# A decoder step on one core: the down projection of pair 0 of the second and third token group is computed from seven products in place of eight

## The chip, the cores and the metric

The kernel runs on one core of a Trainium2 chip. The metric is the device time of one execution in microseconds (us); less is better. TensorE is called PE here, its weight loads PEld, VectorE DVE, ScalarE ACT, GpSimd POOL; SP is the queue from which nearly all transfers (DMAs) are issued.

## What is computed

One layer of a hybrid decoder for 2048 prompt tokens and 8 sample tokens of width 1024: a norm, one input projection, a gated linear recurrence and a sliding-window attention side by side, one output projection, and then the part that matters here, the feed-forward layer with its residual and a last norm:

```python
hn = _rmsnorm(h, norm2_g)
ff = jax.nn.silu(jnp.einsum('btd,df->btf', hn, w_gate)) * jnp.einsum('btd,df->btf', hn, w_up)
y = h + jnp.einsum('btf,fd->btd', ff, w_down)
...
y_prompt = _rmsnorm(yp, final_norm_g)
```

`w_gate` and `w_up` are 1024 x 2816, `w_down` is 2816 x 1024, all fp32.

## The kernel before, in words

**Arithmetic.** Every fp32 operand of a large matmul is split into a high part (`hi`, a cast by ACT to fp32r) and the rest (`lo`, a subtraction by DVE or POOL), and a product is three matmuls: hi x hi, hi x lo, lo x hi. A "product" below means these three, over however many 128-wide pieces of the contraction it has.

**Tiling of the feed-forward layer.** The 2056 tokens are cut into three token groups `gi` = 0, 1, 2 (first, second, third) of 688, 684 and 684 tokens, each of two halves `n` of 344 or 342 (`HALVES`, L35). The 22 slices of 128 of the inner width are taken as 11 pairs `p` = 0 to 10 (`NPAIR`). For every group and pair, `products` (L1360) computes gate (`x` = "g") and then up ("u") as a 2 x 2 block product (two slices by two token halves, the contraction cut in two as well) in Strassen-Winograd form: seven block products in the order `PRODS` = 1, 2, 6, 5, 7, 3, 4, each 12 matmuls, in place of eight. The four blocks of gate go through silu, those of up are multiplied with them; that gives the blocks `(h, n)` (slice h, half n) of the activation, in the tiles `c_u` (pool `gpb`, four buffers, so those of one pair).

**The down projection of a pair** adds its share to the group's result `y` (8 output slices `m` by two halves `n`, in SBUF). It exists in two forms, and `wino(gi, p)` (L77) chooses:

- `down` (L1449): eight products. For each of 16 `(m, n)` two slices x three matmuls, 96 matmuls in all, into a PSUM bank `pd`, and one DVE addition (L1469) into `y`: 16 additions. Its weights are four quarters of 128 x 512 (`down_weights` L1283: a load of 256 KB, a cast by ACT at L1224, a subtraction by POOL at L1225), its activations the four blocks, split by `part` (L1380 ACT, L1381 DVE) into `fh`/`fl`.
- `down_parts` (L1478): seven products, in 14 "rounds" `n` (two per weight tile, order `DPRODS` = 1, 5, 6, 3, 7, 2, 4 for the output slices of half 0, m = 0, 1 and 4, 5, then again for m = 2, 3 and 6, 7). A round is 2 x 3 matmuls into banks `pw` and two DVE additions (L1500): 84 matmuls and 28 additions. Products 1 and 6, then 7, then 4 add up in the same two banks (X), 5 and 3 in two others (Z); 2 has its own. Before the next product may be added to a bank, the addition that reads the bank must be done. Product 1 and 2 go into the y of m = 0, 1 and half 0; 6 and 3 into m = 0, 1 and half 1; 5 and 7 into m = 4, 5 and half 1; 4 into m = 4, 5 and half 0. Seven activations are needed: T1, T2, T3 are blocks, T5, T6, T7, T4 are made from them (L1399, L1402, L1403, L1406) by POOL or DVE (`E_T1`, `E_T2`). T1, T2, T3, T5 are split into the `fh`/`fl` tiles, T6, T7, T4 into two tiles `t`.
- The weights of the seven-product form are made in the second group by `down_make` (L1299: loads of the quarters, sums of them at L1326 by POOL or DVE as `E_DSUM` says, then `split_parts` L1291: cast L1293, subtraction L1294 by `E_DLO1`), and five of the seven tiles are also stored to DRAM (`sums_d`, L1343), from where `down_load` (L1345) takes them in the third group.

In the kernel before, the first group uses eight products for every pair; the second and third use seven for pairs 1 to 9 and eight for pairs 0 and 10.

**Storage around a change of group.** The pool `bigp` has 16 buffers (L303), each of three pieces of 344 columns. A group needs eight of them for a part of its input (`hn`), six for `y` (16 pieces), and two for its `t` tiles. The next group's `y` (loaded from DRAM by `y_load`, L1214 to L1220, in the order m = 0 n = 0, m = 0 n = 1, m = 1 n = 0, ...) and its `t` tiles can only move into buffers that have been left: those of `hn` after its last product, those of the old `y` when `finish` (L1502) has normalised it (L1520, DVE) and its store `out_yT` (L1521) has landed. Both run during pair 1 of the next group.

**What sets the order.** Each step is a Python generator that yields the planned time at which it is due; `plan` (L81) computes these times for the feed-forward layer: 1.764 us per product (`U_M`), 13.927 us for a `down` (`U_D`), 0.875 us per round (`U_R`). In `plan`, the `down` of pair p - 1 stands between gate and up of pair p; where pair p - 1 has seven products, its rounds stand two behind each product of pair p from the third on (`R_AT` = 2, counted from zero). The planned times are priorities: within them, an instruction takes its place on its engine when its operands and buffers are there in a modelled timeline. A written-out order of PE (`PE_ORDER`) covers all up to pair 1 of the first group and nothing behind it.

Of the kernel before, what the change touches and what calls it, by code (L numbers as in the profile page):

```python
# [36 lines left out]
NPAIR = NF // 2  # L37
# [13 lines left out]
T_B0 = 558.156  # L51
T_H3, D_H3 = T_B0 + 38, 4.0
DPRODS = [1, 5, 6, 3, 7, 2, 4]
U_R, R_AT = 0.875, 2
L_RW, L_DR, L_DS = 14.919, 18.881, 9.266
F_LEAD = [9.424, 18.27, 9.0, 0.611, 1.375, 5.911, 3.831, 7.271, 0.408]
F_HN = [23.685, 18.407, 28.406]
# [17 lines left out]


def wino(gi, p):  # L77
    return gi > 0 and 0 < p < NPAIR - 1


def plan():  # L81
    t, begin, end, prod, down, rounds = T_B0, [], [], {}, {}, {}
    for gi in range(len(HALVES)):
        begin.append(t)
        for p in range(NPAIR):
            mixed = p and wino(gi, p - 1)
            n = 0
            for i in range(14):
                if i == 7 and p and not mixed:
                    down[gi, p - 1] = t  # L90
                    t += U_D
                prod[gi, p, "gu"[i // 7], i % 7] = t - (U_D if gi and not p and i < N_EARLY else 0)
                t += U_M
                if mixed and i >= R_AT:
                    for n in range(n, min(14, n + 2)):
                        rounds[gi, p - 1, n] = t
                        t += U_R
                    n += 1
        down[gi, p] = t + (N_EARLY * U_M if gi < len(HALVES) - 1 else 0)
        t += U_D  # L100
        end.append(t)
    return begin, end, prod, down, rounds


T_B, T_END, T_PROD, T_DOWN, T_ROUND = plan()
AFTER = [
    ("xl2_5", "xc1_2_3"), ("xt3_1", "pth5_1_1"),
# [180 lines left out]
def hybrid_step(tc, xT, xR, vecs, cst, gatew, win, wout, wgate, wup, wdown, kT, vC, ck, cv, sconv, sh0,  # L288
# [4 lines left out]
    with ExitStack() as ctx:  # L293
# [884 lines left out]
        with ExitStack() as bctx:  # L1178
# [181 lines left out]
            def products(gi, p, x):  # L1360
# [9 lines left out]
                if not up:  # L1370
                    gss[gi, p] = C
                c11, c12, c21, c22 = (C[h, n][:, :nn] for h in range(2) for n in range(2))
                combine = up and wino(gi, p)
                if combine and gi not in extra:
                    place = slots(bigp, "big", f"t{gi}", F32R)
# [224 lines left out]
            for gi in range(len(HALVES)):  # L1600
                tb = T_B[gi]
                if gi:
                    ch.add(hn_mix(gi, stage, T_MIX[gi], F_MIX[2 * gi - 1]))
                    ch.add(hn_load(gi, PRODS[:3], slots(bigp, "big", f"hn{gi}_0", F32R), tb - F_HN[0], U_M))
                ch.add(hn_load(gi, PRODS[3:], slots(hnp, "hn", f"hn{gi}_1", F32R), tb - F_HN[1], U_M, None if gi else stage))
                ch.add(y_load(gi, tb + F_HN[2]))
                for i, n in enumerate((1, 0)):
                    te = T_END[gi]
                    ch.add(finish(gi, n, te + F_FIN[0] + F_FIN[1] * i, 1.0) if gi < 2 else finish_last(n))
                for p in range(NPAIR):  # L1610
                    ch.add(mixed_weights(wgate, gi, p, "g"))
                    ch.add(mixed_weights(wup, gi, p, "u"))
                    ch.add((down_load if gi == 2 else down_make)(gi, p) if wino(gi, p) else down_weights(gi, p, T_DOWN[gi, p]))
                    ch.add(products(gi, p, "g"))
                    ch.add(products(gi, p, "u"))
                    ch.add((down_parts if wino(gi, p) else down)(gi, p))
# [113 lines left out]
```

## Time and profile before

| | |
|---|---|
| time, three runs | 2064.38, 2058.54, 2060.22 us (median 2060.22) |
| span of the profiled execution | 2054.6 us |
| what lies around the span, against the median | 5.6 us |
| PE / PEld / DVE / ACT / POOL busy | 98% / 93% / 71% / 46% / 44% |
| matmul groups of the feed-forward layer | gate 489.4 us, up 479.9 us, down in eight products (`pd`) 239.4 + 153.4 us, down in seven (`pw`) 165.6 + 126.7 + 91.9 us (matmuls overlap, so these add up to more than the time they take) |
| granted TensorE clock, mean | 0.997 |

The trace has only the span of the profiled execution; the three times come from other executions. A row of the trace that groups instructions has the line, the engine, the operation, what it writes and reads, shape, count, then the busy time in us and the mean duration of one in ns, and behind the second bar the idle time of that engine just before them and what ended it. A row by stretches has for each engine its busy time and the number of instructions, then the granted clock, the share of time that the transfers keep the DMA engines busy, and their rate. A row of the timeline has start, length, engine, line, operation, names and count.

### The profile page before, as it was taken

What the parts mean: (1) busy time and instruction counts of PE and PEld (TensorE: products, weight loads), DVE (VectorE), ACT (ScalarE), POOL (GpSimd) and SP (SyncE); (2) the same over time, 40 slices, a digit from 0 to 9 for tenths busy, and PEclk for the clock granted to TensorE, in tenths of its full rate; (3) what the DMA queues carried; (4) which work ended last, traced back from release to release, by engine and by line L of the source; (5) the groups of instructions that cost most, each with busy time, mean ns of one, the idle gap of its engine ahead of it and who ended that gap; (6) DMA issues with size and microseconds to landing.
All of it is one profiled execution on the core that took longest, in us unless ns stands there. A gap on an engine that the chain in (4) does not pass through costs nothing.

```text
span 2054.6 us, 34857 instructions
## 1 busy us (share of the span) xinstructions
PE 2015.9 (98%) x12319; PEld 1908.1 (93%) x12319; DVE 1459.9 (71%) x2694; ACT 944.6 (46%) x1960; POOL 906.5 (44%) x799
## 2 busy tenths in 40 slices
PE   9999999999999999999999999999999999999998
PEld 9988787878777899999999999999999999999998
DVE  6877886767985766666654667777768666777675
ACT  6764774553664543343334533333335433433343
POOL 5311342020122787567656645556457522322333
PEclk9999999999999999999999999999999999999999
DMA  9864584576688856666546677776677675566652
GB/s 329 293 213 143 188 275 159 175 233 210 208 261 280 314 200 223 205 210 207 207 172 210 229 260 258 227 229 221 222 253 265 211 251 189 183 197 196 197 179 96
DMA packets 208991, 450.98 MB, mean 219 GB/s; under 512 B 25232, under 2 KB 82720, under 8 KB 208800
## 3 DMA queue, kind: packets, MB, share of 16 engines
q1 hardware_dynamic: 205184, 445.73, 65.2%
q10 hardware_dynamic: 3632, 3.02, 0.4%
q8 instruction: 97, 1.59, 0.3%
q14 instruction: 78, 0.64, 0.1%
HBM read 335.89 MB, written 113.84 MB: 219 GB/s over the span
## 4 chain that ended last, share of the span: by engine, by line
PE 77%; DVE 9%; DMA 6%; ACT 3%; issue 2%; POOL 1%; SPq 0%; DVEq 0%; ACTq 0%; POOLq 0%
PE ps_u L396 19%; PE ps_g L396 19%; PE pw L396 11%; PE pd L396 10%; PE ip L396 10%; PE op L396 4%; DMA n<-hs 3%; DMA xs<-in_xT 1%; DMA m<-mixed 1%; PE o L396 1%; PE pt L401 1%; DVE sc L974 1%; DVE sc L963 1%; PE s L396 1%; DMA mixed<-n 1%
## 5 line engine op out<-in xcount | busy, mean ns | idle before, releaser
L396 PE MATMUL ps_g<-hn,w_g 128*128 128x342 f32 (+1 forms) x2772 | 489.4, 320 | 4.6 <-DVE c_u L1410 1.8
L396 PE MATMUL ps_u<-hn,w_u 128*128 128x342 f32 (+1 forms) x2772 | 479.9, 319 | 1.9 <-ACT c_u L1436 1.3
L396 PEld LDWEIGHTS ps_g<-hn,w_g 128*128 128x128 f32 x2772 | 445.1, 188 | 6.0 <-DVE c_u L1410 2.3
L396 PEld LDWEIGHTS ps_u<-hn,w_u 128*128 128x128 f32 x2772 | 444.2, 188 | 2.6 <-ACT c_u L1436 1.6
L396 PE MATMUL ip<-xn,w_in 128*128 128x512 f32 (+1 forms) x1680 | 353.4, 358 | 1.9 <-ACT xn L431 1.8
L396 PEld LDWEIGHTS ip<-xn,w_in 128*128 128x128 f32 x1680 | 270.1, 189 | 46.0 <-issue 3.8
L1500 DVE TENSOR_TENSOR y<-y,pw 128x342 f32<-128x342 f32 x504 | 238.7, 504 | 73.0 <-PE pw L396 72.2
L396 PE MATMUL pd<-fh,w_d 128*128 128x344 f32 (+1 forms) x960 | 239.4, 320 | 0.6 <-DVE y L1469 0.6
L396 PE MATMUL op<-mix,w_out 128*128 128x512 f32 (+1 forms) x960 | 203.4, 357 | 0.5 <-DVE rrec L763 0.3
L396 PEld LDWEIGHTS op<-mix,w_out 128*128 128x128 f32 x960 | 155.4, 188 | 29.3 <-issue 5.0
L1469 DVE TENSOR_TENSOR y<-y,pd 128x344 f32<-128x344 f32 (+1 forms) x240 | 117.9, 507 | 75.3 <-PE pd L396 70.7
L396 PEld LDWEIGHTS pd<-fh,w_d 128*128 128x128 f32 x960 | 168.3, 188 | 1.4 <-DVE y L1469 1.1
L396 PE MATMUL pw<-fh,wd 128*128 128x342 f32 x576 | 165.6, 319 | 1.2 <-DVE y L1500 1.2
L396 PE MATMUL pd<-fl,w_d 128*128 128x344 f32 (+1 forms) x480 | 153.4, 320 | 0.0
L1381 DVE TENSOR_TENSOR fl<-c_u,fh 128x342 fp32r<-128x342 f32 (+1 forms) x132 | 107.1, 815 | 48.3 <-ACT fh L1380 47.9
L1225 POOL TENSOR_TENSOR w_u<-ru,w_u 128x512 fp32r<-128x512 f32 x44 | 58.9, 1338 | 181.6 <-ACT w_u L1224 155.0
L1392 POOL TENSOR_TENSOR c_u<-c_u,c_g 128x342 f32<-128x342 f32 (+1 forms) x60 | 60.5, 1008 | 170.7 <-DVE c_u L1410 132.1
L1380 ACT CAST fh<-c_u 128x342 fp32r<-128x342 f32 (+1 forms) x132 | 63.0, 480 | 157.8 <-POOL c_u L1392 61.9
L396 PE MATMUL pw<-t,wd 128*128 128x342 f32 x648 | 126.7, 320 | 2.6 <-DVE t L1381 1.7
L1410 DVE TENSOR_TENSOR c_u<-c_u,ps_u 128x342 f32<-128x342 f32 (+1 forms) x99 | 50.2, 507 | 100.3 <-PE ps_u L396 100.1
L396 PEld LDWEIGHTS pw<-t,wd 128*128 128x128 f32 x648 | 106.0, 188 | 4.4 <-DVE t L1381 2.5
L396 PEld LDWEIGHTS pw<-fh,wd 128*128 128x128 f32 x576 | 105.3, 189 | 1.7 <-DVE y L1500 1.5
(316 smaller groups left out, 3507.4 us busy)
## 6 DMA issues: line engine op xcount, KB each, us to landing
w_g<-split_g SPq DMA_DIRECT2D x88, 512.0 KB, 4.2
w_u<-split_u SPq DMA_DIRECT2D x88, 512.0 KB, 4.9
w_in<-split_w SPq DMA_DIRECT2D x84, 512.0 KB, 3.5
rg<-in_wgate SPq DMA_DIRECT2D x110, 256.0 KB, 3.1
ru<-in_wup SPq DMA_DIRECT2D x110, 256.0 KB, 3.2
w_out<-split_w SPq DMA_DIRECT2D x48, 512.0 KB, 4.4
split_g<-w_g SPq DMA_DIRECT2D x44, 512.0 KB, 3.6
split_u<-w_u SPq DMA_DIRECT2D x44, 512.0 KB, 2.7
```

The lines of the kernel that those rows point to most:

```text
L396: r = nc.tensor.matmul(*args, **kw)
L401: r = nc.tensor.transpose(*args)
L963: seen[f"sm{gb}_{kv}_{g}"] = nc.vector.tensor_tensor_reduce(sc[:, g, :kn], ps[:, gi * 256:gi * 256 + kn], mask[:, k0:k0 + kn], -SCALE, ns[ ...
L974: nc.vector.tensor_scalar(sc[:, g, :kn], sc[:, g, :kn], mx[:, 1, g:g + 1], None, ALU.mult)
L1225: lo_eng.tensor_tensor(w[:, 1, :], src, w[:, 0, :].bitcast(F32), op=ALU.subtract)
L1380: nc.scalar.copy(hi, v)
L1381: nc.vector.tensor_tensor(lo, v, hi.bitcast(F32), ALU.subtract)
L1392: (nc.vector if p == NPAIR - 1 or src is not v else eng(E_MUL[2 * h + n])).tensor_tensor(v, src, g, op=ALU.mult)
L1410: nc.vector.tensor_tensor(o, a, b, op)
L1469: r = nc.vector.tensor_tensor(ys[gi, n, m], ys[gi, n, m], ps, ALU.add)
L1500: nc.vector.tensor_tensor(v, v, ps, ALU.add)
```

## The change

`wino` now also holds for pair 0 of the second and third group, so these two `down` become `down_parts`, with all that belongs to it: `down_make` or `down_load` for their weights, the T activations in `products`, the rounds. In `plan`, the rounds of pair 0 stand behind the seventh to the thirteenth product of pair 1 (`R_FIRST` = 6), which puts the first of them at the planned time that the `down` had. All planned times behind them move forward, by 1.677 us per group.

```diff
-U_R, R_AT = 0.875, 2
+U_R, R_AT, R_FIRST = 0.875, 2, 6
...
 def wino(gi, p):
-    return gi > 0 and 0 < p < NPAIR - 1
+    return gi > 0 and p < NPAIR - 1
...
-                if mixed and i >= R_AT:
+                if mixed and i >= (R_AT if p > 1 else R_FIRST):
                     for n in range(n, min(14, n + 2)):
                         rounds[gi, p - 1, n] = t
                         t += U_R
```

## The prediction

> **What bounds the kernel now.** I read the page first, then the stretches by pair, then PE's waits, then the timelines of SP, DVE and PE around the change of group.
>
> ```profile
> span 2054.6 us, 34857 instructions
> PE 2015.9 (98%) x12319; PEld 1908.1 (93%) x12319; DVE 1459.9 (71%) x2694; ACT 944.6 (46%) x1960; POOL 906.5 (44%) x799
> ```
>
> PE is busy throughout, so a matmul removed is time removed, unless PE then waits. The span is 2054.6 us; against the median of the runs, 2060.22, there lie 5.6 us around it, which the change does not touch. I sum against the span and add the same 5.6.
>
> The stretches (start:end, length, then busy time and count of PE, PEld, DVE, ACT, POOL) of one pair with eight products (first group, pair 5), one with seven in its place (third group, pair 4), then pair 1 of the second and of the third group, where the change falls:
>
> ```profile
> 872.70:914.20 41.50, 41.50 (x265) 41.50 (x265) 28.48 (x42) 16.30 (x32) 26.93 (x20) 1.00 0.62 210
> 1742.10:1781.70 39.60, 39.60 (x255) 39.60 (x254) 27.86 (x52) 14.96 (x30) 11.54 (x10) 1.00 0.64 199
> 1166.70:1211.20 44.50, 44.50 (x297) 44.49 (x296) 26.00 (x49) 13.59 (x28) 16.22 (x16) 1.00 0.79 266
> 1620.80:1662.90 42.10, 42.10 (x278) 42.10 (x277) 25.82 (x51) 13.20 (x26) 11.43 (x10) 1.00 0.78 248
> ```
>
> PE never rests in any of the four, and its clock is full. Where PE does wait, second group and then third:
>
> ```profile
> PE pw L396 <- DVE y L1500: 2.0, 3, 1.2
> PE ps_g L396 <- DVE c_u L1410: 1.8, 2, 0.9
> PE pw L396 <- DVE t L1381: 1.7, 3, 1.1
> PE ps_u L396 <- ACT c_u L1436: 1.3, 1, 1.3
> ...
> PE pd L396 <- DVE y L1469: 0.6, 2, 0.3
> ```
>
> That is 6.8 us in the second group and 0.6 in the third, most of it behind DVE.
>
> **What goes: matmuls.** By the code a pair with seven products has 84 + 84 + 84 = 252 matmuls, with eight 264. 39.60 / 252 = 0.157 us each, and the first two stretches differ by 1.9 us = 12 x 0.157. The change does this in two groups: 2 x 1.9 = **-3.8 us**. [...]
>
> **What comes, engine by engine.**
>
> ```profile
> L1500 DVE TENSOR_TENSOR y<-y,pw 128x342 f32<-128x342 f32 x504 | 238.7, 504 | 73.0 <-PE pw L396 72.2
> L1469 DVE TENSOR_TENSOR y<-y,pd 128x344 f32<-128x344 f32 (+1 forms) x240 | 117.9, 507 | 75.3 <-PE pd L396 70.7
> L1381 DVE TENSOR_TENSOR t<-c_u,t 128x342 fp32r<-128x342 f32 x54 | 44.3, 829 | 3.3 <-ACT t L1380 3.3
> L1294 DVE TENSOR_TENSOR wd<-rd,wd 128x512 fp32r<-128x512 f32 x54 | 51.7, 957 | 2.7 <-ACT wd L1293 2.7
> L1225 POOL TENSOR_TENSOR w_d<-rd,w_d 128x512 fp32r<-128x512 f32 x60 | 86.3, 1446 | 25.2 <-ACT w_d L1224 24.8 <-POOL w_d L1225 0.4
> L1294 POOL TENSOR_TENSOR wd<-rd,wd 128x512 fp32r<-128x512 f32 x45 | 61.0, 1355 | 77.3 <-ACT wd L1293 63.2 <-DVE y L1500 12.4 <-DVE c_u L1392 1.7
> L1326 POOL TENSOR_TENSOR sd<-rd,sd 128x256 f32<-128x256 f32 x18 | 17.6, 976 | 0.8
> L1406 POOL TENSOR_TENSOR c_u<-c_u,c_u 128x342 f32<-128x342 f32 x18 | 19.3, 1074 | 12.1 <-DVE fl L1381 11.6
> ```
>
> DVE, second group: 28 additions in place of 16 (12 x 0.504 = 6.0), three more T remainders (3 x 0.829 = 2.5), three weight remainders (3 x 0.957 = 2.9), one sum (under 1): +12 us; third group about +13 (four weight remainders, one T). Pairs 0 and 1 hold it: in pair 1 alone DVE idles 44.5 - 26.0 = 18.5 and 42.1 - 25.8 = 16.3 us. POOL, second group: -4 x 1.446 + 4 x 1.355 + 7 x 0.976 + 4 x 1.074 = +10.7 us, beside 28.3 idle in pair 1; third about +1. ACT: three casts of weights and three of T more, about 3 us beside 30 idle. SP gets five more stores and six more loads (ten halves of a quarter in place of four quarters) in the second group, four more loads in the third, at about half a us each (eight stores take 5.10 and 4.13 below), spread over the 25 us ahead of the stores of y. In sum all of this is covered by idle time; each such us costs one if the cover is gone at the moment PE needs the result.
>
> **The wait that the change brings.** SP's loads of the new y, second group and then third:
>
> ```profile
> 1124.94 0.62 SPq L1220 DMA_DIRECT2D y<-hs  x1
> 1136.86 4.17 SPq L1220 DMA_DIRECT2D y<-hs  x5
> ...
> 1191.22 0.53 SPq L1343 DMA_DIRECT2D sums_d<-sd  x1
> 1193.28 0.80 SPq L1220 DMA_DIRECT2D y<-hs  x2
> 1194.13 5.10 SPq L1521 DMA_DIRECT2D out_yT<-y  x8
> 1199.31 0.42 SPq L1220 DMA_DIRECT2D y<-hs  x1
> 1200.34 3.26 SPq L1220 DMA_DIRECT2D y<-hs  x7
> ...
> DMA to landing us min/median/max: 1.9/4.1/4.7
> ...
> DMA to landing us min/median/max: 4.3/4.5/6.9
> ...
> 1644.53 4.13 SPq L1521 DMA_DIRECT2D out_yT<-y  x8
> 1648.93 3.39 SPq L1220 DMA_DIRECT2D y<-hs  x7
> ```
>
> Six pieces of y (m = 0 to 2) come early, ten only around 1193 to 1204, seven of them behind the store of the old y. (The two landing rows are those of the stores and of the loads.) PE is already at this down projection:
>
> ```profile
> 1178.64 0.32 PE L396 MATMUL pd<-fh,w_d 128*128 128x342 f32 x1
> ...
> 1633.30 0.32 PE L396 MATMUL pd<-fh,w_d 128*128 128x342 f32 x1
> ```
>
> Eight products use y in the order in which it comes, so only late additions wait. Seven products change that in two ways. First, the second round (product 5) adds into m = 4, 5 of half 1, the 10th and 12th piece; product 3 must follow it in the same banks, so round four stands until about 1205. Second, T6, T7 and T4 of pair 0 need the group's two t tiles now, one pair earlier, and the 16 buffers are taken (8 hn, 6 old y, 2 new y): the first comes when the first buffer of the old y is stored, 1191.1 + 4.1 = 1195, the second after the second store of the other block, about 1196 + 4.1 = 1200, and T7 is split some 2 us later, 1202. Till then `c_u` of pair 0 holds its buffers, and up of pair 1 gets no further than its fourth product, since products 7 and 3 need banks that are copied into `c_u`.
>
> What PE can do meanwhile from 1178.6: 48 matmuls of gate (7.5 us), norm matmuls (about 2), four products of up (7.5), rounds 1, 2, half of 6 (15 matmuls, 2.4) and round 3 (0.9), in sum 20.3 us, to about 1199. So PE waits 1199 to 1202: **+2.7 us**. Behind that lie three products of up and a round (6.6 us), which cover y of 1205. Bounds: 0 if the stores go out 3 us sooner (DVE no longer has to slip the old additions between the normalisations), 8 if T4 and the late y are waited for in full (1207). Third group: work from 1633.3 to about 1651, T7 at 1644.5 + 1 + 4.1 + 1.8 = 1651.4: **+0.4 us**, bounds 0 and 4. I take the middle estimates, since the rows of before place each step.
>
> Sum: 2054.6 - 3.8 + 2.7 + 0.4 = 2053.9 of span, with 5.6 around it **2059.5 us**. A measurement of this kernel can tell about 0.3% from no change, 6.2 us; -0.7 us lies well within.
>
> **The rivals.**
>
> Clean gain: PE finds work over the whole wait, as it does now (44.50 of 44.50 busy in that stretch although ten pieces of y are late). For it: the order behind the first group is not written out, and PE takes what is ready. Against it: the products of pair 2 need weight buffers that the standing rounds hold. 2060.2 - 3.8 = 2056.4 us.
>
> Slower: a jam at the change of group. T tiles, `c_u` buffers and late y hold one another, and when they come free at 1202 to 1207, some 24 additions, ten T remainders and the new weights fall on DVE at once, 12 + 8 + 5 us of DVE work before the 20 us of PE work that waits for it. Price: 8 + 4 for the full waits, 2 to 5 for the burst (the pairs of the second group that wait at all wait 1 to 3 us each), -3.8: 2070 us. It decides if the waits exceed 3.8 + 6.2 = 10 us. What DVE's share is worth depends on these rows:
>
> ```profile
> L1381 DVE TENSOR_TENSOR fl<-c_u,fh x132: 500/793/1658, 706.1 to 2026.1; 128x342 fp32r<-128x342 f32 x88, 128x344 fp32r<-128x344 f32 x44
> L1500 DVE TENSOR_TENSOR y<-y,pw x504: 494/503/515, 1220.6 to 2017.6; 128x342 f32<-128x342 f32 x168
> ```
>
> The addition from PSUM always takes 0.50, the remainder of two SBUF operands 0.50 to 1.66; ten remainders at the upper end are 8 us more. [...]
>
> Faster: the waits that the second group already has (6.8 us) fall otherwise once every later step has moved, and most of them go: 2056.4 - 3 to 6.8, about 2051 us. The stretches show no reason for it, only that such waits come and go from pair to pair.
>
> The change does not do what it says: the seventh product is only a planned time. The first pd ran when gate of pair 1 had four products to go. The rounds may be spread into pair 2, and the 12 matmuls saved all the same, 2056 to 2062 us.
>
> **How the numbers follow.** The forecast 0.42, clean gain 0.26, jam 0.18, faster 0.08, rounds elsewhere 0.06. The first, second and last lie within 0.3%: 0.74 the same. Of the jam nearly all is over 6.2 us: slower 0.17 (the rest goes to the same), faster 0.08, same 0.75. The range goes from 2054.5, just under the clean gain and what a run scatters, to 2067, the waits at their bounds without the burst and half of the jam: it leaves out the faster case and the upper half of the jam, under 0.2.
>
> **What would show it.** Right: 24 fewer matmuls in 2 x 1.9 us; pw from about 1178 and 1633 on; `t` tiles written from about 1196 and 1646; waits of PE of 1 to 5 us near 1199 to 1203, released by DVE or ACT on `c_u`; POOL longer by 10 us in the second group. Wrong: waits over 10 us between 1195 and 1230, or pairs 2 and 3 of the second group longer than 40 us by DVE; or no wait, and then the clean gain.

## The result, and the profile after

| | before | after |
|---|---|---|
| time, median (four runs each) | 2061.78 us (2058.54 to 2064.38) | 2091.91 us (2090.93 to 2093.09) |
| ratio after / before | | 1.0142, 95% interval 1.0125 to 1.016 |
| span of the profiled execution | 2054.6 us | 2090.9 us |

The change makes the kernel 1.4% slower, 30 us by the medians and 36.3 us by the two spans. The forecast was 2059.5 us, no change. (The ratios, here and below, differ a little from the quotient of the medians, which is 1.0146 here; the intervals are those of the ratios.)

The page of the profile after, its span and its busy times:

```profile
span 2090.9 us, 34921 instructions
PE 2026.9 (97%) x12295; PEld 1913.6 (92%) x12295; DVE 1483.5 (71%) x2733; ACT 948.9 (45%) x1972; POOL 921.4 (44%) x812
```

The work changed as forecast: 24 matmuls fewer (12319 to 12295), DVE 23.6 us longer (12 + 13 were counted), POOL 14.9 (11.7 counted), ACT 4.3. What grew is the time in which PE has nothing to do. The stretches after (length, then busy time and count of PE, PEld, DVE, ACT, POOL, then granted clock, DMA share, GB/s) of pair 1 and pair 2 of the second group and pair 1 of the third:

```profile
1169.80:1222.20 52.40, 44.18 (x276) 42.77 (x276) 32.31 (x55) 15.98 (x34) 23.71 (x23) 0.93 0.71 227
1222.20:1268.20 46.00, 43.45 (x263) 42.55 (x262) 35.38 (x63) 15.08 (x30) 26.98 (x26) 0.96 0.72 243
1649.60:1696.80 47.20, 41.58 (x251) 39.77 (x250) 32.79 (x62) 15.39 (x32) 14.66 (x12) 0.93 0.76 242
```

Pair 1 had 44.50 of 44.50 us busy before; now 8.2 of 52.4 us are idle, and in the third group 5.6 of 47.2. DVE is at 62% and 69% there, so it isn't full. PE's waits in pair 1, second group and then third:

```profile
PE pw L396 <- DVE y L1500: 7.1, 3, 4.7
PE ps_u L396 <- DMA w_u<-split_u: 1.1, 1, 1.1
...
PE pw L396 <- DVE y L1500: 5.6, 4, 1.8
```

PE waits for an addition into `y` that frees a bank, and for a weight of up. The addition in turn waits, as DVE's timeline in that stretch says (in brackets the idle time before the row and what ended it):

```profile
1204.23 0.51 DVE L1500 TENSOR_TENSOR y<-y,pw 128x342 f32<-128x342 f32 x1 [2.34 <-DMA y<-hs]
1207.19 0.51 DVE L1500 TENSOR_TENSOR y<-y,pw 128x342 f32<-128x342 f32 x1 [2.45 <-DMA out_yT<-y]
1209.68 1.55 DVE L1500 TENSOR_TENSOR y<-y,pw 128x342 f32<-128x342 f32 x3 [1.98 <-DMA y<-hs]
```

So the loads of the new `y` are late. SP's timeline shows how late, and what stands behind them:

```profile
1186.89 0.33 SPq L1248 DMA_DIRECT2D w_u<-split_u  x1
...
1189.82 4.83 SPq L1521 DMA_DIRECT2D out_yT<-y  x8
1194.77 1.34 SPq L1220 DMA_DIRECT2D y<-hs  x3
...
1196.63 3.96 SPq L1521 DMA_DIRECT2D out_yT<-y  x6
1201.72 2.23 SPq L1220 DMA_DIRECT2D y<-hs  x5
1203.99 0.90 SPq L1521 DMA_DIRECT2D out_yT<-y  x2
1204.94 4.84 SPq L1220 DMA_DIRECT2D y<-hs  x8
...
1210.35 0.85 SPq L1248 DMA_DIRECT2D w_u<-split_u  x2
...
1216.91 0.40 SPq L1248 DMA_DIRECT2D w_u<-split_u  x1
```

All 16 pieces of `y` come after 1194, where six came by 1141 before. And between the load of a weight of up at 1186.89 and the next ones at 1210.35 lie 23.5 us, filled with stores and loads that SP issues one behind another, loads of `y` among them that wait for stores of `y` (2.0 us in all); in the kernel before, four weights of up went out between 1188.12 and 1204.77, among the stores and loads of `y`. The first and the last of these four:

```profile
1188.12 0.40 SPq L1248 DMA_DIRECT2D w_u<-split_u  x1
...
1204.45 0.32 SPq L1248 DMA_DIRECT2D w_u<-split_u  x1
```

Of the 23.5 us, 18.1 are the issue of 16 stores and 16 loads of `y`, and for some 4 SP stands idle. What is late is the issue and not the transfer itself: the loads of `y` land 3.5 us after their issue here (2.7 to 4.1), where those of the same stretch took 4.4 before. Why `y` lost its early buffers is in the rows of the `t` tiles, before and after (count, then shortest/median/longest ns, first and last start):

```profile
L1380 ACT CAST t<-c_u x54: 461/479/482, 1221.0 to 1993.2; 128x342 fp32r<-128x342 f32 x54
```

```profile
L1380 ACT CAST t<-c_u x60: 462/480/483, 1180.2 to 2029.2; 128x342 fp32r<-128x342 f32 x60
```

The `t` tiles are first written at 1180, before any old `y` has been stored: they took the two buffers that `y` had. (e11 below gives these buffers back to `y` and so tests this.)

To add up where the time went I use the starts of all matmuls of the trace: where two of them in succession lie over 0.2 us apart, what exceeds the usual 0.158 us counts as a gap. A gap holds waits, and matmuls that run slower behind a wait (behind the 4.71 us wait of pair 1 they start 0.285 us apart for 3.4 us). By stretch, in us:

```
                                   before   after   difference
pair 1, second group                 0.3     11.4     +11.1
pair 1, third group                  0.3      9.6      +9.3
pairs 2 to 9, second group           8.3     23.4     +15.1
rest of the feed-forward layer      12.0     15.9      +3.9
sum                                 20.9     60.3     +39.4
```

39.4 less the 3.8 us of the matmuls is 35.6, and the spans differ by 36.3. So there are two places to explain: pair 1 of both groups (+20.4), and pairs 2 to 9 of the second group (+15.1), in which nothing was changed but planned times.

### The profile page after: what moved, and what is told of

It is laid out like the page before. It is cut to its first block, busy times and chain, and to the rows that moved or that the text cites. A ratio compares the mean times of both kernels' runs of the same rounds, so it can differ in the third digit from the quotient of the medians.

```text
span 2090.9 us, 34921 instructions
## 1 busy us (share of the span) xinstructions
PE 2026.9 (97%) x12295; PEld 1913.6 (92%) x12295; DVE 1483.5 (71%) x2733; ACT 948.9 (45%) x1972; POOL 921.4 (44%) x812
## 4 chain that ended last, share of the span: by engine, by line
PE 70%; DVE 10%; DMA 9%; ACT 3%; issue 3%; POOL 3%; SPq 1%; ACTq 0%; DVEq 0%; POOLq 0%
PE ps_u L396 17%; PE ps_g L396 16%; PE pw L396 10%; PE ip L396 9%; PE pd L396 9%; PE op L396 5%; DMA n<-hs 4%; DMA mixed<-n 1%; DMA out_yT<-y 1%; DVE n L521 1%; PE o L396 1%; PE s L396 1%; PE pt L401 1%; DVE sc L963 1%; DMA rd<-in_wdown 1%
## 5 line engine op out<-in xcount | busy, mean ns | idle before, releaser
L1500 DVE TENSOR_TENSOR y<-y,pw 128x342 f32<-128x342 f32 x560 | 265.1, 504 | 93.4 <-PE pw L396 77.8
L396 PE MATMUL pd<-fh,w_d 128*128 128x344 f32 (+1 forms) x832 | 206.6, 320 | 1.4 <-DVE y L1469 1.4
L396 PE MATMUL pw<-fh,wd 128*128 128x342 f32 x640 | 189.0, 327 | 10.3 <-DVE y L1500 10.1
L396 PE MATMUL pw<-t,wd 128*128 128x342 f32 x720 | 145.0, 326 | 15.4 <-DVE y L1500 9.5
L1469 DVE TENSOR_TENSOR y<-y,pd 128x344 f32<-128x344 f32 (+1 forms) x208 | 103.2, 508 | 65.6 <-PE pd L396 65.3
L396 PEld LDWEIGHTS pd<-fh,w_d 128*128 128x128 f32 x832 | 145.8, 188 | 1.9 <-DVE y L1469 1.6
L1381 DVE TENSOR_TENSOR fl<-c_u,fh 128x342 fp32r<-128x342 f32 (+1 forms) x132 | 105.5, 803 | 49.1 <-ACT fh L1380 48.5
L396 PEld LDWEIGHTS pw<-t,wd 128*128 128x128 f32 x720 | 120.0, 192 | 19.4 <-DVE y L1500 12.3
L396 PE MATMUL pd<-fl,w_d 128*128 128x344 f32 (+1 forms) x416 | 133.1, 321 | 0.0
L396 PEld LDWEIGHTS pw<-fh,wd 128*128 128x128 f32 x640 | 120.0, 193 | 13.1 <-DVE y L1500 12.9
```

The lines of the kernel that those rows point to most:

```text
L396: r = nc.tensor.matmul(*args, **kw)
L1381: nc.vector.tensor_tensor(lo, v, hi.bitcast(F32), ALU.subtract)
L1469: r = nc.vector.tensor_tensor(ys[gi, n, m], ys[gi, n, m], ps, ALU.add)
L1500: nc.vector.tensor_tensor(v, v, ps, ALU.add)
```

## The experiments

The theories, as they stood: **Y**: `y` is late since the `t` tiles take its two spare buffers. **D**: DVE is late with the additional additions, remainders and splits around pair 1. **Q**, formed after e8: beside `y`, the weights of up are late, because they stand in SP's queue behind the loads of `y`, which wait for stores. **N**, formed after e12: pairs 2 to 9 wait because the norm that prepares the third group's input keeps its planned time while the pairs move forward. All results are in this table; the gaps are those of the profiled execution, worked out as above (the column "pairs 2 to 9" is that of the second group). That is one execution of each kernel, and not always one near the median: 2101.52 us in e3, 2081.68 in e1. In pair 1 of the second group, kernels that are alike there agree within 0.5 us (0.3 in before, e2, e14, e16 and e17; 2.1 to 2.2 in e11, e13 and e18; 5.0 and 5.5 in e12 and e15).

```
                              time us    ratio    95% interval        gaps, us: pair 1   pairs    pair 1
                              (median)                               2nd group  2 to 9  3rd group
before                        2058.7 to 2062.5, by chip                 0.3       8.3     0.3
after                         2091.91   1.0142   1.0125 to 1.016       11.4      23.4     9.6
e1  second group only         2088.44   1.0120   1.0099 to 1.0142      11.2      21.6     0.9
e2  third group only          2070.05   1.0039   1.0024 to 1.0054       0.3      13.7     8.7
e3  no y                      2093.47   1.0157   1.0131 to 1.0183      10.8      25.3     9.7
e4  own t tiles               2094.78   1.0161   1.0143 to 1.018       10.0      24.8     5.5
e5  before, small pools       2080.84   1.0101   1.0084 to 1.0118       2.6      19.1     1.6
e6  own t tiles, y order      2098.31   1.0179   1.0163 to 1.0196      12.8      28.3     1.9
e7  rounds later              2088.53   1.0140   1.0122 to 1.0157      10.3      23.7     7.9
e8  y order                   2086.77   1.0128   1.0108 to 1.0147      13.7      16.9     9.1
e9  no y, y loaded later      2069.43   1.0035   1.0024 to 1.0046       0.3      16.5     2.5
e10 up's weights from ACT     2087.80   1.0121   1.0095 to 1.0146       5.0      23.2     8.9
e11 y first                   2082.52   1.0097   1.0078 to 1.0116       2.1      29.7     4.6
e12 e11, weights from ACT     2079.53   1.0087   1.0063 to 1.0111       5.0      21.3     2.5
e13 e11, norm earlier         2070.78   1.0049   1.0029 to 1.0069       2.2      21.8     1.3
e14 before, norm later        2071.73   1.0045   1.003  to 1.0061       0.3      15.9     0.3
e15 e12, norm earlier         2075.73   1.0070   1.0046 to 1.0093       5.5      20.6     2.2
e16 e2, y first               2065.71   1.0023   1.0006 to 1.0039       0.3      13.4     5.1
e17 before, norm earlier      2062.41   1.0013   0.9999 to 1.0027       0.3      10.1     0.3
e18 e13, norm earlier still   2068.52   1.0049   1.0036 to 1.0062       2.2      17.0     1.7
```

### e1 and e2: one group at a time

```diff
-    return gi > 0 and p < NPAIR - 1
+    return gi > 0 and (gi == 2) <= p < NPAIR - 1      # e1; e2 has (gi == 1)
```

In e2 the weights of pair 0 are made in the third group (`down_make`), since the second group has stored none.

> Pair 0 in seven products in the second group alone; the third group as before. Theory Y (PE waits for the new y, whose pieces come late because the two t tiles of pair 0 now hold the two spare buffers of the pool): the waits of pairs 0 to 2 of the second group stay (16 us, against 1 before), about +14 us after the 1.9 saved; the 11 us more of waits in pairs 4 to 9 of that group stay too if they follow from it, so 2075 to 2086 us, and the third group loses its 10 us of waits. Theory D (DVE has too much to do around pair 1): the same split, since both groups get the same DVE work; this run does not tell Y from D but says where the 30 us come from.

> Pair 0 in seven products in the third group alone, with its weight sums made there; the second group as before. If each group carries its own loss: about 10 us of waits against 1.6, less 1.9, so +8 us, 2068 to 2072 us; and pairs 4 to 9 of the second group wait 8 us as before. If those pairs wait 18 us here as well, the extra 11 us there do not come from the second group's pair 0.

The second group alone costs 2088.44 - 2061.48 = 27 us, the third alone 8.6. In e1 the waits are nearly those of the changed kernel: 11.2 us in pair 1 and 21.6 in pairs 2 to 9. In e2 they are 8.7 us in pair 1 of the third group. The third group has no later group whose input must be prepared, and nothing follows there: its pairs 2 to 9 have gaps of 0.0 in e2 as in the kernel before.

### e3: pair 0 doesn't add into y

```diff
-    nc.vector.tensor_tensor(v, v, ps, ALU.add)
+    if p:
+        nc.vector.tensor_tensor(v, v, ps, ALU.add)
+    else:
+        nc.vector.tensor_tensor(ps, hn[gi, 1, 0][0][:, :nn].bitcast(F32), ps, ALU.add)
```

> As changed, but the 28 additions of each pair 0 add a resident input tile to the bank and write it back there, in place of adding the bank into y; this leaves out the share of pair 0 of the second and third group in the result. The DVE instructions, their number and their place behind the matmuls stay; only y is no longer waited for. Theory Y: the waits in pair 1 and 2 go from 16 to under 4 us in the second group and from 10 to under 3 in the third, 2058 to 2068 us. Theory D: nothing goes, 2085 to 2093 us.

No gain at all: 2093.47 us, and 10.8 us of gaps in pair 1 of the second group. Theory Y by itself has fallen. But PE's waits of that stretch, second group and then third, name another culprit:

```profile
PE ps_u L396 <- DMA w_u<-split_u: 7.5, 1, 7.5
...
PE ps_u L396 <- DMA w_u<-split_u: 6.2, 1, 6.2
```

What was a wait of 1.1 us behind 7.1 us is now one of 7.5 us. Two things were late by nearly the same time, and the trace puts a wait down to the one that came last. SP's timeline of e3:

```profile
1192.63 0.33 SPq L1248 DMA_DIRECT2D w_u<-split_u  x1
...
1211.47 4.58 SPq L1220 DMA_DIRECT2D y<-hs  x8
1216.15 0.85 SPq L1248 DMA_DIRECT2D w_u<-split_u  x2
```

Nobody waits for `y` in pair 1 here, but its loads still stand ahead of the weights.

### e4, e5 and e6: own tiles for T6, T7 and T4

```diff
-    place = slots(bigp, "big", f"t{gi}", F32R)
+    place = slots(tsp, "ts", f"t{gi}", F32R, 3 * TP)     # e4, e6: tsp has 2 buffers
-rwp2 = B(tc.tile_pool(name="rwp2", bufs=4))              # e4, e5, e6: with 3 in rwp, a ring of 7 raw weights,
-wp2 = B(tc.tile_pool(name="wp2", bufs=3))                # and with 5 in wp one of 8 split weights
+rwp2 = B(tc.tile_pool(name="rwp2", bufs=2))              # 5 and 7
+wp2 = B(tc.tile_pool(name="wp2", bufs=2))
```

The two tiles are paid for with weight buffers; e5 is the kernel before with those small rings alone. e6 also loads `y` in the order in which the rounds want it (as e8).

> As changed, but the t tiles have two buffers of their own, so that the new y gets the two spare buffers of the pool again; to make room, the pools of raw and of split weights lose two buffers and one (7 to 5, 8 to 7), which the control run prices. Theory Y: six pieces of y come early again, ten at about 1195 to 1205; round two still waits for the 10th and 12th piece at about 1205 in place of 1209 to 1212: 5 to 8 us come back in the second group and 3 to 6 in the third, 2078 to 2084 us, plus what the smaller pools cost. Theory D: no change, 2090 us or more.

> Control: the kernel before with the smaller pools of raw and split weights (5 and 7 buffers), nothing else. All theories: what it is slower than the kernel before is the price of the smaller pools; 2060 to 2075 us.

> As the run with own t tiles, and y is loaded in the order in which the rounds use it (m = 0, 1 of half 0, m = 4, 5 of half 1, m = 0, 1 of half 1, m = 4, 5 of half 0, then the same with m = 2, 3, 6, 7), so that the six early pieces serve the first six rounds. Theory Y: PE has the first half of the rounds before the late pieces land; the waits of pair 1 fall below 4 us in the second group and 2 in the third, and the time comes to the control's less 0 to 4 us. Theory D: as the run with own t tiles.

As times these are lost: the small rings cost the kernel before 1.0%, and neither e4 nor e6 says what own tiles are worth in the second group. e6 was expected at the time of e5 or a little below; it came 17 us above. The third group can be read: its pair 1 goes from 9.6 us of gaps to 5.5 (own tiles) to 1.9 (and y order), where the rings by themselves (e5) leave 1.6. There Y holds. In the second group of e6 the wait is again `PE ps_u <- w_u`, 8.0 us.

### e7: the rounds behind the last products

```diff
-U_R, R_AT, R_FIRST = 0.875, 2, 6
+U_R, R_AT, R_FIRST = 0.875, 2, 9
-                    for n in range(n, min(14, n + 2)):
+                    for n in range(n, min(14, n + (2 if p > 1 else 3))):
```

The last round of pair 0 then stands behind the last product of pair 1, which has written its own T4 into the tile that both pairs share: the product 4 that goes into m = 6 and 7, half 0, is that of a wrong block. The work is the same in kind and number.

> As changed, but the rounds of pair 0 are planned three behind each product of pair 1 from the tenth on, in place of two from the seventh on: some 5 us later. Theory Y: PE does more products of up before it meets the rounds, if the buffers of c_u and of weights allow; 3 to 10 us come back, 2082 to 2088 us. Theory D: a denser burst of additions, no gain or a loss, 2090 to 2097 us. A third, that the planned place matters little since PE takes what is ready: within 2 us of the changed kernel.

The first round is planned three products later (5.3 us), and the ratio stays: 1.0140 for 1.0142. But the plan moved more than the rounds did. By the matmul starts, the first round of the second group still begins 14.5 us into pair 1, the second at 24.8 us (17.4 in the changed kernel) and the sixth, behind the long wait, at 41.7 (40.5). So this shift of the planned times brings nothing; it doesn't show that the place of the rounds is without weight.

### e8: y in the order of the rounds

```diff
-                for m in range(KD):
-                    yield t + m
-                    for n, (o, nn) in enumerate(HALVES[gi]):
+                first = ((0, 0), (1, 0), (4, 1), (5, 1), (0, 1), (1, 1), (4, 0), (5, 0)) if gi else ()
+                first += tuple((m + 2 * (gi > 0), n) for m, n in first)
+                for i, (m, n) in enumerate(first or [(m, n) for m in range(KD) for n in range(2)]):
+                    yield t + i // 2
+                    o, nn = HALVES[gi][n]
```

> As changed, with y loaded in the order in which the rounds use it and nothing else. Theory Y: the first pieces to land (three near 1198, the next from 1205) are then those that rounds one and two need; round two no longer waits for the 10th and 12th piece at 1209 to 1212 but for the 3rd and 4th: 5 to 12 us come back in the second group and 3 to 6 in the third, 2074 to 2084 us. Theory D: 2090 us.

A ratio of 1.0128, little less than after, and pair 1 of the second group even has 2.3 us more. PE's waits there:

```profile
PE ps_u L396 <- DMA w_u<-split_u: 7.0, 1, 7.0
PE pw L396 <- DVE y L1502: 3.0, 3, 1.9
```

The wait for `y` has shrunk from 7.1 to 3.0 us, and the one for up's weight has taken its place, as in e3. From this row theory Q was formed, and its test: undo both at once.

### e9: no y, and its loads out of the way

e3, and

```diff
-    ch.add(y_load(gi, tb + F_HN[2]))
+    ch.add(y_load(gi, tb + F_HN[2] + (25 if gi else 0)))
```

(The share of pair 0 of the second and third group is left out, as in e3.)

> The changed kernel, with the additions of pair 0 (second and third group) not into y, as in e3 (its share of the result is left out), and the loads of the new y of those groups planned 25 us later. Nothing of pair 1 reads y now, and SP's queue has no y loads ahead of up's weights. Theory Q (up's last weight for pair 1 stands in SP's in-order queue behind loads of y that wait for stores): the 7.5 us wait of PE for w_u in e3 goes, pair 1 of the second group waits under 4 us in place of 10.8, and the time falls by 5 us or more below e3's 2093.5, to about 2086 to 2088. Theory D (DVE is late with additions, remainders and splits around pair 1): the same 10 us wait behind DVE, 2092 to 2095.

2069.43 us, 24 us less than e3, from nothing but the planned time of loads that no one waits for in pair 1. That is far more than expected (2086 to 2088): by the table, the gaps of the third group's pair 1 fall too, by 7.2 us, and those of pairs 2 to 9 by 8.8. Pair 1 of the second group has gaps of 0.3 us, as before the change. SP's timeline:

```profile
1191.04 4.83 SPq L1524 DMA_DIRECT2D out_yT<-y  x8
1196.95 0.41 SPq L1248 DMA_DIRECT2D w_u<-split_u  x1
...
1208.21 8.15 SPq L1220 DMA_DIRECT2D y<-hs  x14
```

Two weights of up go out at 1197 and 1198, in place of 1216. All the additional DVE work of pair 0 is still there, so D has fallen for pair 1, and Q is shown. (The 2.5 us left in the third group's pair 1 are a wait for a weight of up, 2.0 us, and not for DVE.) That `y` is late beside it, the rows of the changed kernel show in the second group (DVE behind `y<-hs`), and e4 and e6 in the third.

### e10: up's weights from another queue

e8, and

```diff
-    nc.sync.dma_start(w.bitcast(F32), split_s[x][p, SPLIT.index(r)])
+    (nc.scalar if p == 1 and x == "u" else nc.sync).dma_start(w.bitcast(F32), split_s[x][p, SPLIT.index(r)])
```

> The changed kernel with the y order of e8, and the stored weights of up for pair 1 of the second and third group (4 loads each) issued from ACT's queue in place of SP's. Theory Q: the 7.0 us wait of PE for w_u in the second group goes; what is left of its 13.7 us is the y wait of 3 us and small ones, 5 to 7 us; the time falls from e8's 2086.8 to about 2079 to 2082, and the third group, where y alone is late, stays at 9. If ACT's queue then stands for a weight buffer as long as SP's did, or the wait is DVE's: no change, 2085 to 2088.

Half right. The wait for w_u is gone and pair 1 falls from 13.7 to 5.0 us, as Q says. The time doesn't fall (2087.80): pairs 2 to 9 have 23.2 us of gaps in place of 16.9. What is won in one place is lost there; by what, this run doesn't say.

### e11: y first

e8, and

```diff
-                    yield t + i // 2
+                    yield t + i // 2 - (20 if gi and i < 6 else 0)
```

> The changed kernel with the y order of e8 and the first six pieces of the new y planned 20 us earlier, so that y takes the two spare buffers, as the prediction had it, and the t tiles move into buffers of the old y. The prediction's estimate for just this case was 2.7 us of wait in the second group and 0.4 in the third (bounds 8 and 4). If that estimate was sound and only the premise (who gets the spare buffers) was wrong: pair 1 waits at most 8 us in the second group in place of 13.7 and at most 4 in the third in place of 9.1, and the time is 2075 to 2080. Theory Q: the third group gains (its y is there), but in the second up's weights stay behind the y loads in SP's queue, with 7 to 13 us of wait, 2080 to 2085. If t tiles were what matters: both waits stay, released by DVE or ACT on t.

This is the case that the prediction had reckoned with, six pieces of `y` early and `t` tiles in buffers of the old `y`, but for one thing: `y` also comes in the order of the rounds here, which the prediction didn't have. SP's timeline, and then ACT's, for the casts into the `t` tiles:

```profile
1125.22 1.25 SPq L1222 DMA_DIRECT2D y<-hs  x2
1135.66 1.18 SPq L1222 DMA_DIRECT2D y<-hs  x2
1138.98 1.91 SPq L1222 DMA_DIRECT2D y<-hs  x2
...
1194.41 0.41 SPq L1250 DMA_DIRECT2D w_u<-split_u  x1
...
1195.38 0.38 SPq L1250 DMA_DIRECT2D w_u<-split_u  x1
```

```profile
1193.50 0.86 ACT L1382 CAST t<-c_u 128x342 fp32r<-128x342 f32 x2 [0.75 <-DMA out_yT<-y]
1202.72 0.48 ACT L1382 CAST t<-c_u 128x342 fp32r<-128x342 f32 x1 [1.09 <-DMA out_yT<-y]
```

The two `t` buffers come free at 1193.5 and 1202.7 (the prediction had 1195 and 1200), and PE's waits in pair 1, second group and then third, are these:

```profile
PE ps_u L396 <- ACT c_u L1438: 0.7, 1, 0.7
PE pw L396 <- DVE y L1502: 0.6, 1, 0.6
...
PE ps_u L396 <- ACT c_u L1438: 1.9, 1, 1.9
```

Gaps of pair 1: 2.1 and 4.6 us, where 2.7 and 0.4 stood in the prediction. Q's own expectation for this run, 7 to 13 us in the second group, was wrong: with ten loads of `y` left and none of them urgent, two weights of up slip ahead of the second group of stores. In time the run brings 2082.52: pairs 2 to 9 now have 29.7 us of gaps.

### e12: both

e11 with the diff of e10.

> e10 and e11 together: y order, first six pieces early, up's weights for pair 1 from ACT's queue. Theory Q with theory Y in the third group: both causes of the wait are gone, pair 1 waits under 5 us in the second group and under 4 in the third, the time is 2068 to 2074; the rest over 2061.7 lies in pairs 4 to 9 of the second group. Theory D: 2083 or more.

2079.53, above what was expected; pair 1 5.0 and 2.5 us. ACT's queue is no gift either. From here on the open question is pairs 2 to 9.

### e13, e14 and e15: the norm's place

While the second group runs, the input of the third is normalised in steps (`hn_mix`: a load of `hs`, a DVE multiplication L521, sums L529, a store). These steps are planned from the start of the second group, `T_B[1]`. The change moves pairs 2 to 10 forward by 1.677 us against that start, and so against the norm.

```diff
-T_MIX = [None, T_B[0] + F_MIX[0], T_B[1] + F_MIX[2]]
+T_MIX = [None, T_B[0] + F_MIX[0], T_B[1] + F_MIX[2] - 1.677]     # e13 from e11, e15 from e12
+T_MIX = [None, T_B[0] + F_MIX[0], T_B[1] + F_MIX[2] + 1.677]     # e14 from the kernel before
```

> e11 (y first), and the planned start of the norm that prepares the third group's input moved 1.677 us earlier, so that it stands against pairs 2 to 10 of the second group as in the kernel before. Theory N (the plan's norm steps, whose loads DVE waits for, fall on other rounds once the pairs have moved): the waits of pairs 2 to 9 fall from 29.7 us to 8 to 14 and the time from 2082.5 to 2060 to 2068. If these waits come from what pair 1 left behind, or from many small shifts of order: 20 or more stay, 2076 to 2085.

> The kernel before, with nothing changed but the planned start of the same norm, 1.677 us later: the shift against the pairs that the change brings, alone. Theory N: pairs 2 to 9 of the second group wait 15 us or more in place of 8.2, and the time rises by 7 us or more, to 2069 or more. If the shift is harmless: 2060 to 2064.

> e12 (y first, up's weights for pair 1 from ACT's queue) with the norm's start put back as in e13. Theory N: 2058 to 2066. Otherwise 2074 to 2082.

e14 is the cleanest of all. The kernel before with one planned time moved by 1.677 us loses 0.45% (0.3 to 0.61), 9 us, and its pairs 2 to 9 have 15.9 us of gaps in place of 8.3. The stretches of these pairs, before and then e14:

```profile
1211.20:1536.40 325.20, 319.64 (x2019) 316.65 (x2018) 242.25 (x424) 118.60 (x240) 187.47 (x170) 1.00 0.71 232
```

```profile
1212.00:1545.00 333.00, 322.10 (x2019) 318.08 (x2018) 244.47 (x423) 117.70 (x241) 186.31 (x170) 0.99 0.69 226
```

The same matmuls take 7.8 us longer. How, the longest wait of e14 shows, in DVE's and then PE's timeline:

```profile
1493.59 0.60 DVE L521 SCALAR_TENSOR_TENSOR n<-n,vec,hb 128x342 f32<-128x342 f32 x1 [4.20 <-DMA n<-hs]
1494.22 1.07 DVE L529 TENSOR_TENSOR n<-n,n 128x342 f32<-128x342 f32 x2
1495.20 1.77 DVE L1500 TENSOR_TENSOR y<-y,pw 128x342 f32<-128x342 f32 x4
```

```profile
1489.51 0.80 PE L396 MATMUL ps_u<-hn,w_u 128*128 128x342 f32 x4
...
1495.76 1.51 PE L396 MATMUL pw<-t,wd 128*128 128x342 f32 x4 [2.62 <-DVE y L1500]
```

DVE stands idle for 4.2 us, until a load of the norm has landed, with four additions queued behind it, for which PE waits 2.62 us. The first four matmuls behind this wait take 1.51 us, where four took 0.80 ahead of it. The wait and these four make some 3.3 us (2.62 + 0.71) of the 7.6 that the gaps have grown by; the rest lies in the matmuls behind them and in smaller waits. DVE waits for such loads as long in the kernel before (29.3 us in these pairs, 30.4 in e14); what differs here is what is queued behind them at that moment. In the changed kernel there is also the case without a load: at 1414.06 PE has waited 4.26 us for a remainder of T, and DVE's timeline ahead of it reads

```profile
1408.10 1.42 DVE L1294 TENSOR_TENSOR wd<-rd,wd 128x512 fp32r<-128x512 f32 x1
1409.44 1.58 DVE L1381 TENSOR_TENSOR t<-c_u,t 128x342 fp32r<-128x342 f32 x1
1410.94 1.57 DVE L529 TENSOR_TENSOR n<-n,n 128x342 f32<-128x342 f32 x1
1412.43 1.57 DVE L1381 TENSOR_TENSOR t<-c_u,t 128x342 fp32r<-128x342 f32 x1
```

four instructions of two SBUF operands in a row, one of them the norm's. The last three are near the upper end of their ranges (1.6 us; L529 0.49 to 1.61, L1381 on `t` 0.50 to 1.61).

e13 takes 10 us off e11 (the ratio goes from 1.0097 to 1.0049), with 21.8 us in pairs 2 to 9 in place of 29.7; 8 to 14 and at most 2068 were expected, so N is right in its direction and not the whole. e15 is 3.5 us better than e12 by the ratios, which lies within their intervals, and is also short of what was expected.

### e16: the third group alone, with y first

e2 with the edits of e8 and e11.

> The change in the third group only (e2, with pair 0's weights made there), with y order and the first six pieces early. If y alone was late there: pair 1 of the third group waits under 5 us in place of 8.7 and the time falls from e2's 2070.1 to 2063 to 2066; the second group's waits stay at 12 to 16 us in sum, since its schedule differs from before only by what is planned later.

2065.71 us, by the ratios 3.3 below e2, though their intervals overlap; pair 1 of the third group 5.1 us, a hair over the 5 expected. The other columns are nearly those of e2. It is the best of the changed kernels, and still slower than before by 0.06 to 0.39%.

### e17 and e18: is the order of before a special point?

```diff
+T_MIX = [None, T_B[0] + F_MIX[0], T_B[1] + F_MIX[2] - 1.677]     # e17 from the kernel before
+T_MIX = [None, T_B[0] + F_MIX[0], T_B[1] + F_MIX[2] - 3.354]     # e18 from e11
```

> The kernel before, with only the planned start of the third group's norm 1.677 us earlier (e14 had it later: pairs 2 to 9 of the second group waited 15.0 us in place of 8.2). If the order of before is a point found by trying, which any shift loses: 12 us or more there again, and 2066 to 2072. If only a late norm hurts: 6 to 10 us, 2058 to 2064.

> e13 with the norm another 1.677 us earlier (3.354 in all against e11). If the changed kernel only wants the norm earlier: pairs 2 to 9 wait 14 us or less in place of 21.7 and the time falls under 2066. If it is a matter of which order falls out: 18 to 30 us and 2069 to 2082, as likely worse than e13 as better.

(The 15.0 us in the first expectation leave out pair 9; with it e14 has 15.9.) The kernel before doesn't mind an earlier norm: 10.1 us of gaps, ratio 1.0013 with 1 in its interval. So not any shift hurts: of the two tried on the kernel before, the later norm costs 9 us and the earlier one nothing that shows. e18 has the ratio of e13, with 17.0 us of gaps, between the two expectations: an earlier norm doesn't give the rest back.

## Why the prediction was wrong

**What held.** The matmuls went as counted, 24 of them at an unchanged distance (0.157 us). DVE's and POOL's additional work was within some 3 us of its sum. `pw` begins 14.5 and 12.6 us into pair 1 of the two groups (1184.3, 1662.2), where `pd` began 11.9 and 12.5 us into it. The waits did come at the change of group and lie where the text had said it would be wrong: 11.4 us of gaps in pair 1 of the second group, 8.2 of them idle time, where it had named over 10 us between 1195 and 1230; and pair 2 of that group, with 46.0 us, is longer than 40.

**"The 16 buffers are taken (8 hn, 6 old y, 2 new y)".** This is the step that failed first. The row of before showed who held the two spare buffers then, and I let `y` keep them. The `t` tiles are wanted one pair earlier now, and they got them; all 16 pieces of `y` then stood behind the stores of the old `y`. Under the premise as written (e11) the working holds well in the second group: buffers free at 1193.5 and 1202.7 for 1195 and 1200, 2.1 us of gaps for 2.7. In the third, 4.6 us stand for 0.4, a little over its upper bound of 4; with the norm put back (e13, e18) they are 1.3 and 1.7. How far the working holds for late pieces of `y` in their old order, e11 doesn't say. e4 has six early pieces in that order, and PE still waits 5.6 us for `y` in the second group and 2.9 in the third, though with smaller rings; so nothing here bears out that three products of up and a round cover them. With the premise wrong, the two terms were 11.1 and 9.3.

**The list of SP's transfers, "spread over the 25 us ahead of the stores of y".** I counted the issue time of the additional ones, about half a us each, and saw `y` behind the stores, but not the weights of up behind `y`. With no `y` loaded early, 16 stores and 16 loads stood in one block, 18.1 us of issue time and some 4 of waits, and 23.5 us passed between two weights of up. With `y` out of it, the place of those loads alone was worth 24 us (e3 to e9); taken by itself, neither the wait for `y` (e3) nor that for the weights (e10) brought any time.

**"In sum all of this is covered by idle time."** True of the sum and no use: DVE's 18.5 idle us in pair 1 were not idle at the moment when an addition was due, and pairs 2 to 9, to which the sum gave nothing, lost 15.1 us. Of these a part is the norm's planned place, which the diff doesn't show: moved alone to its later place it costs the kernel before 9 us (e14), and put back it takes 10 us off e11 (e13). In e9, where both waits of pair 1 are gone and the norm is not put back, pairs 2 to 9 have 16.5 us, about what the shift alone makes (15.9). That all planned times behind the change move forward by 1.677 us per group stands in the section on the change; the prediction made nothing of it but that "such waits come and go".

**5.6 us around the span.** The changed kernel's profiled execution took 2092.72 us for a span of 2090.9, so about 1.8 us lie around a span; the rest of the 5.6 was the difference between executions. It moves the forecast by 4 us and decides nothing.

**The rivals.** The jam had the right sign and place, and at 2070 us, 10 above before, a third of the size. Its story was that `t` tiles, `c_u` and `y` hold one another; `t` tiles and `c_u` were in time, and weights of up took their place. Of its 2 to 5 us for the burst on DVE nothing was seen in pair 1 (e9 has all of that work, and gaps of 0.3 us in the second group; the 2.5 in the third are mostly a wait for a weight of up).

**What stays open.** With `y` first and the norm put back, 9 to 14 us more gaps than before remain in pairs 2 to 9 of the second group (e13 21.8, e18 17.0, before 8.3). Other kernels that touch no product there have them as well (e2 13.7, e16 13.4). Whether the rest comes from what pair 1 leaves behind or from an order that merely falls out otherwise, the runs don't tell. No version was found that beats the kernel before.

## What to carry to other kernels

When a step is moved earlier, ask of each shared pool who will now ask first, and not only whether a buffer is free; and for each transfer that it delays, read what is queued behind it: here the next weight, behind 32 transfers of `y`, cost as much as `y` itself (e3 leaves 10.8 of the 11.4 us). If two things are late by about the same time, the trace shows one, and mending one brings nothing: e3 and e8 looked like refutations, and were halves. And a change that moves planned times moves everything against the steps that are planned from elsewhere: look for those, and try that shift alone.

## What the runs showed of the hardware

Behind the 4.71 us wait of pair 1, PE did not resume at full pace. Its timeline in the changed kernel:

```profile
1210.25 0.66 PE L396 MATMUL pw<-fh,wd 128*128 128x342 f32 x1 [4.71 <-DVE y L1500]
...
1212.12 0.49 PE L396 MATMUL pw<-fh,wd 128*128 128x342 f32 x1
1212.41 0.49 PE L396 MATMUL pw<-fl,wd 128*128 128x342 f32 x1
...
1214.28 0.32 PE L396 MATMUL pw<-fh,wd 128*128 128x342 f32 x1
1214.44 0.31 PE L396 MATMUL pw<-fl,wd 128*128 128x342 f32 x1
```

From 1210.25 to about 1213.7 the matmuls follow each other at 0.285 us, behind that at 0.157; the granted clock is 0.50 from 1206.9 to 1213.7 and 1.00 from 1213.8 on. At 0.285 in place of 0.157, these 3.4 us hold about 12 matmuls that lose 0.13 us each: some 1.5 us on top of the wait, which the prediction had not priced. The wait need not be as long as 4.71 us: behind e14's wait of 2.62 us the first four matmuls took 1.51 us, in place of 0.80. Behind one of 2.31 us of the changed kernel, which ends at 1613.66, the granted clock stayed at 1.00 and the next 24 matmuls took 4.06 us. From which length of wait on PE is slower, the runs don't tell.

In SP's queue of the changed kernel no transfer passed one that waited 8.7 us, the longest of SP's waits in pair 1:

```profile
SPq L1248 <- PE ps_g L396: 8.7, 1, 8.7
```

The 8.7 us are a load of up's weights that waits for its buffer, ending with its issue at 1186.89. SP's row ahead of it is a load at 1177.78 (0.33 us), its next one a load at 1188.63, and the first store of `y` follows at 1189.82.
